# Seven products for pairs of MLP up tiles, and the down projection in groups of four hidden tiles

## The chip, the core and the metric

The kernel runs on one core of a Trainium2 chip. What counts is the device time of one execution in microseconds; three runs gave 1147.07, 1148.77 and 1148.97, the median being 1148.77. TensorE (PE in the rows) multiplies, VectorE (DVE) and ScalarE (ACT) work on tiles, GpSimd (POOL) on a few, and SyncE (SP) issues the loads and stores.

## The reference

An encoder trunk of two layers on 512 positions, 1024 channels wide, in float32. Each layer mixes (layer 0 by a gated convolution, layer 1 by differential attention over shared keys and values; both with a 4-head attention over a memory of 256 rows beside it), and then has an MLP of 4096 hidden channels:

```
def sqrelu_mlp(h, w_up, w_down):
    u = jnp.einsum('bsd,df->bsf', h, w_up)
    return jnp.einsum('bsf,fd->bsd', jnp.square(jax.nn.relu(u)), w_down)
...
        x = x + jnp.einsum('bse,ed->bsd', jnp.concatenate([main, mo], axis=-1), w_o[l])
        x = x + sqrelu_mlp(rmsnorm(x, norm_mlp[l]), w_up[l], w_down[l])
```

rmsnorm divides by the root of the mean square over the channels and multiplies by a gain.

## The kernel before

Everything lies transposed, channels on partitions and the 512 positions in the free dimension; the residual stream is 8 tiles x of 128 x 512. To keep float32 accuracy each operand is split into two halves of type fp32r, a rounded part and the rest (wh and wl for weights, xh and xl for activations, hh and hl for hidden tiles), and each product of 128 x 128 weights with a tile is three matmuls into the same PSUM bank: wh by xh, wh by xl, wl by xh (`product`, L276 to L281).

Weights come as a list of units (`_unit_list`), in the order of use, each of up to 8 blocks of 128 x 128. `dma_to` (L225) loads a unit into one of 3 buffers raw. `prep_to` (L251) splits a half unit of 4 blocks: ScalarE copies it to wh (L261), VectorE subtracts to wl (L263). It is called three halves ahead of the matmuls (AHEAD is 3), and there are 4 buffers of wh and of wl. `gemm_pieces` (L283) goes through the 8 blocks of a unit, 24 matmuls in all.

`mlp` (L737) works in 4 quarters of 8 hidden tiles. A quarter has 8 up projections and then 8 down projections:

```
                dve.scalar_tensor_tensor(out=v, in0=ps, scalar=0.0, in1=rstd, op0=ALU.max, op1=ALU.mult)
                act.activation(out=hh, in_=v, func=AF.Square)
                act.activation(out=a, in_=v, func=AF.Square)
                dve.tensor_tensor(out=hl, in0=a, in1=hh.bitcast(F32), op=ALU.subtract)
```

(L762 to L765) for each up tile, where rstd is the inverse root of the norm, applied behind the product; the norm's gain is in xh and xl already. A down unit accumulates the 8 hidden tiles of the quarter in one bank, and L772 adds it to x. At the end of the first MLP each x tile is split for the next layer and its square added up (`norm_tile` L430, `norm_square`; on GpSimd, the last one on VectorE: L455); the sum is split into ah and al (`norm_split`), and `norm_root` (L464) has TensorE add it over the partitions (L467, L468). In layer B the weights of attention are first multiplied by the norm's gain on GpSimd (L244).

The W_o stage of layer 0 adds to x (L882) and splits it for the MLP (L435, L436). In the second MLP the first two up tiles are done together (`side`). `mem_keys` and `mem_values` work on the 256 memory rows, thus with matmuls of 256 columns. PSUM's 8 banks are 3 for `gbank`, 1 in pn and 4 in pm_. The code gives each engine its instructions and the tile framework places them in the engines' queues: a queue's order is the framework's, which need not be that of the code.

Of the kernel before, what the change touches and what calls it, by code (L numbers as in the profile page):

```python
# [22 lines left out]
NF = 4  # L23
# [30 lines left out]

LAYER_B = ([(0, t) for t in range(6)] + [(1, t) for t in range(5)] + [(2, t) for t in range(4)]
# [8 lines left out]
def _unit_list():  # L64

    u = []
    u += [("qmA", t, KT) for t in range(2)]
    for m in range(NH):
        if m == MEMA:
            u += [("mkv", 0, t, KT) for t in range(4)]  # L70
        if m == MEMB:
            u += [("mkv", 1, t, KT) for t in range(4)]
        u += [("win", CONV + m * P, KT), ("win", 2 * CONV + m * P, KT), ("win", m * P, KT)]
    u += [("woA", d, KT) for d in range(KT)]

    def mlp(l):
        r = []
        for q in range(NF):
            r += [("up", l, q * KT + f, KT) for f in range(KT)]
            r += [("dn", l, q, d, KT) for d in range(KT)]  # L80
# [12 lines left out]
    return u  # L93
# [8 lines left out]
def _pack_weights(a_w_in, b_w_q, w_kv, w_mem_kv, w_o, w_up, w_down):  # L102
    wall = np.empty(OFFS[-1], np.float32)

    def cols(w, c0):
        return w[:, c0 : c0 + P].reshape(-1, P, P).transpose(1, 0, 2)

    for u, off in zip(UNITS, OFFS):
        kind = u[0]
        if kind == "qmA":  # L110
            b = cols(a_w_in[0], 3 * CONV + u[1] * P)
        elif kind == "win":
            b = cols(a_w_in[0], u[1])
        elif kind == "mkv":
            b = cols(w_mem_kv[u[1]], u[2] * P)
        elif kind == "woA":
            b = cols(w_o[0], u[1] * P)
        elif kind == "up":
            b = cols(w_up[u[1]], u[2] * P)
        elif kind == "dn":  # L120
            b = cols(w_down[u[1]][u[2] * D : (u[2] + 1) * D], u[3] * P)
# [12 lines left out]
        wall[off : off + n] = np.ascontiguousarray(b).reshape(-1)  # L134
    return wall
# [56 lines left out]
def trunk_kernel(ctx: ExitStack, tc: tile.TileContext, xT, memT, wall, cst, shp, csn, out):  # L192
# [11 lines left out]
    xspool = mk("xspool")  # L204
    hpool = mk("hpool", 8)
    qpool = mk("qpool", 16)
    ptpool = mk("ptpool")
# [10 lines left out]
    halves = [(i, h) for i, u in enumerate(UNITS) for h in range((u[-1] + SEG - 1) // SEG)]  # L218
# [6 lines left out]
    def dma_to(n, between=()):  # L225
        between = list(between)
        while st["dma"] <= min(n, len(UNITS) - 1):
            i = st["dma"]
            kind, nb = UNITS[i][0], UNITS[i][-1]
            r = wpool.tile([P, KT, P], F32, tag="raw", name="raw", bufs=3)  # L230
# [19 lines left out]

    def prep_to(n):  # L251
        while st["prep"] <= min(n, len(halves) - 1):
            i, h = halves[st["prep"]]
            dma_to(i + 1)
            r = st["raw"][i]
            b0, b1 = h * SEG, min(UNITS[i][-1], h * SEG + SEG)
            rs = r[:, b0:b1, :]
# [84 lines left out]
    def gbank():  # L342
        return pg.tile([P, S], F32, tag="g", name="g")
# [16 lines left out]

    def load_consts():
# [7 lines left out]
    def load_shape_consts():  # L369
        ind = tpool.tile([P, 512], F32, tag="att", name="ind", bufs=2)  # L370
# [59 lines left out]
    def norm_tile(k, src, g0, w, hi, lo, squares=True):  # L430
# [6 lines left out]
        if squares:  # L437
            norm_square(k, src, w)

    def norm_square(k, src, w, eng=None, by=None, tags=("sqf",)):  # L440
# [6 lines left out]
        if k == 0:  # L447
            nrm["acc"] = tpool.tile([P, S], F32, tag="vt", name="acc")
            square(nrm["acc"][:, :w])
        else:  # L450
# [3 lines left out]
            eng = eng or (dve if k == KT - 1 else pool)  # L454
# [87 lines left out]
    def mem_queries(hn, srcs, rstd, layer):  # L542
        def one(t):
            ps = gbank()
            yield from gemm_pieces(ps, srcs)
# [39 lines left out]
    def mem_attention(mq, mkk, mv, mixer, pace):  # L585
        def rest(T, hp, pr_):
            yield pace[1]
            th = ptpool.tile([P, 4, M], F32R, tag="p1h", name="mth")
            tl = ptpool.tile([P, 4, M], F32R, tag="p1l", name="mtl")
# [20 lines left out]
        for T in range(2):  # L610
            for hp in range(2):
# [9 lines left out]
                pr_ = tpool.tile([P, 4, M], F32, tag="att", name="mp", bufs=2)  # L621
# [35 lines left out]
    def diff_attention(p, qk, vv, mixer, done):  # L657
        obs, pts = {}, {}

        def rest(h, i, pm):  # L660
# [6 lines left out]
            if il == 0:  # L667
                th = ptpool.tile([P, nj, M], F32R, tag=f"p{T}h", name="th")
                tl = ptpool.tile([P, nj, M], F32R, tag=f"p{T}l", name="tl")
# [29 lines left out]
        def softmax(h, i, sc):  # L699
# [6 lines left out]
            pm = tpool.tile([P, 2, S], F32, tag="att", name="pm", bufs=2)  # L706
# [24 lines left out]

    def hid_pair():
        return (hpool.tile([P, S], F32R, tag="hh", name="hh"), hpool.tile([P, S], F32R, tag="hl", name="hl"))

    kept = []

    def mlp(l, xs, xs_next):  # L737
        rstd = new_rstd()
        parts = norm_split(S) if l == 0 else None
        for q in range(NF):  # L740
            hid = []
            ahead = {}
            for f in range(KT):
# [9 lines left out]
                if q == 0 and f == 0:  # L753
                    if parts is None:
                        for d in range(KT):
                            norm_square(d, x[d], S, tags=("sqf", "saf", "ob", "rp"))
                        parts = norm_split(S)
                    norm_root(parts, S, rstd)
                v = qpool.tile([P, S], F32, tag="q", name="v")
                a = qpool.tile([P, S], F32, tag="q", name="a")  # L760
                hh, hl = hid_pair()
                dve.scalar_tensor_tensor(out=v, in0=ps, scalar=0.0, in1=rstd, op0=ALU.max, op1=ALU.mult)  # L762
                act.activation(out=hh, in_=v, func=AF.Square)  # L763
                act.activation(out=a, in_=v, func=AF.Square)  # L764
                dve.tensor_tensor(out=hl, in0=a, in1=hh.bitcast(F32), op=ALU.subtract)  # L765
                hid.append((hh, hl))
            for d in range(KT):
                last = q == NF - 1 and xs_next is None
                for c in (slice(0, M), slice(M, S)) if last and d == KT - 1 else (slice(0, S),):
                    ps = gbank()  # L770
                    gemm(ps[:, c], hid, cols=c)
                    dve.tensor_tensor(out=x[d][:, c], in0=x[d][:, c], in1=ps[:, c], op=ALU.add)  # L772
                    if last:
                        nc.sync.dma_start(out=out[d * P : (d + 1) * P, c], in_=x[d][:, c])
                if q == NF - 1 and not last:
                    norm_tile(d, x[d], None, S, xs_next[d][0], xs_next[d][1])
                    kept.append(dpool.tile([P, S], F32, tag=f"x{d}", name=f"x{d}"))
                    nc.sync.dma_start(out=kept[d], in_=x[d])
# [100 lines left out]
    for d in range(KT):  # L879
# [3 lines left out]
        norm_tile(d, x[d], C_MLP0, S, xs[d][0], xs[d][1])  # L883
    lam_consts()
    xs_next = xs_tiles()
    mlp(0, xs, xs_next)


    xs = xs_next
    rstd = new_rstd()  # L890
# [5 lines left out]
    q0, q1 = mem_queries(hn, xs, rstd, 1)  # L896
# [125 lines left out]
    mlp(1, x_new, None)  # L1022
# [35 lines left out]
```

## Time and profile before

| | |
|---|---|
| median of three runs | 1148.77 us |
| the profiled execution | 1148.93 us, of which the span 1147.2 |
| TensorE matmuls | 5343, busy 1133.3 us (99%) |
| VectorE, ScalarE, GpSimd busy | 658.0 (57%), 535.2 (47%), 127.4 us (11%) |
| first MLP | 211.4 to 558.3 us |
| second MLP | 791.5 to 1145 us |

A row of a timeline has the start in the span, the duration, the engine and line, and what it writes and reads; in brackets, the idle time of the engine ahead of it and what ended that. A group row has the count, the busy time and the mean duration, and then the idle time before its members. Matmuls overlap: their durations don't add up, their starts do.

### The profile page before, as it was taken

To read this page: it belongs to the slowest core of one execution; us is meant where nothing else is said; L and a number is where in the kernel's file an instruction comes from. 1 tells how busy PE (TensorE), PEld (TensorE's weight loads), DVE (VectorE), ACT (ScalarE), POOL (GpSimd) and SP (SyncE) were. 2 spreads that over 40 slices of the span, in tenths; PEclk is the share of its full clock that TensorE was granted. 3 is DMA by queue.
4 is the path that set the end of the run, shared out by engine and by line. 5 is a ranking of instruction groups with operands and counts; after the bars stand their busy time and mean duration, and the time that the engine had idled before them with its cause. 6 is when DMAs were issued, how large, how long until landed. Compare 5 with 4: busy or idle time off the path is not lost.

```text
span 1147.2 us, 14439 instructions
## 1 busy us (share of the span) xinstructions
PE 1133.3 (99%) x5343; PEld 929.5 (81%) x5343; DVE 658.0 (57%) x1106; ACT 535.2 (47%) x1037; POOL 127.4 (11%) x130
## 2 busy tenths in 40 slices
PE   8999999999999999999999999999999999999998
PEld 6888888888888888888887777777788888888887
DVE  7876664653443443444678899977643443543442
ACT  6656544442342342344577777675532432432431
POOL 3100002000000000002523342224000000000000
PEclk9999999999999999999999999999999999999999
DMA  7232333223322322234322223212322232223231
GB/s 270 97 112 73 103 108 102 92 92 98 104 92 92 107 95 92 95 108 138 120 83 67 63 70 106 93 56 74 99 103 92 93 108 94 92 96 107 93 114 70
DMA packets 38983, 113.64 MB, mean 99 GB/s; under 512 B 4992, under 2 KB 6528, under 8 KB 38912
## 3 DMA queue, kind: packets, MB, share of 16 engines
q1 hardware_dynamic: 38912, 112.71, 29.8%
q8 instruction: 42, 0.69, 0.2%
q14 instruction: 29, 0.24, 0.1%
HBM read 106.93 MB, written 4.19 MB: 97 GB/s over the span
## 4 chain that ended last, share of the span: by engine, by line
PE 85%; DVE 4%; ACT 2%; issue 1%; ACTq 0%; DVEq 0%
PE g L279 26%; PE g L280 26%; PE g L281 26%; PE sc L583 1%; PE mov L603 1%; PE o L690 1%; DVE xl L436 1%; PE mtp L594 1%; DVE wl L263 1%; PE msc L583 0%; PE tp L677 0%; DVE ra L420 0%; DVE dnb L705 0%; DVE x L1018 0%; ACT pm L708 0%
## 5 line engine op out<-in xcount | busy, mean ns | idle before, releaser
L261 ACT ACTIVATE wh<-raw 128x512 fp32r<-128x512 f32 x384 | 241.8, 630 | 482.6 <-PE g L280 422.5
L263 DVE TENSOR_TENSOR wl<-raw,wh 128x512 fp32r<-128x512 f32 x370 | 263.4, 713 | 176.0 <-ACT wh L261 174.7
L279 PE MATMUL g<-xh,wh 128*128 128x512 f32 x816 | 323.4, 397 | 0.4 <-DVE x L1018 0.4
L280 PE MATMUL g<-xl,wh 128*128 128x512 f32 x816 | 320.4, 393 | 1.8 <-DVE xl L436 1.7
L281 PE MATMUL g<-xh,wl 128*128 128x512 f32 x816 | 319.0, 391 | 0.0
L279 PE MATMUL g<-hh,wh 128*128 128x512 f32 (+1 forms) x626 | 243.1, 388 | 0.0
L281 PE MATMUL g<-hh,wl 128*128 128x512 f32 (+1 forms) x626 | 242.2, 387 | 0.0
L280 PE MATMUL g<-hl,wh 128*128 128x512 f32 (+1 forms) x626 | 242.2, 387 | 0.0
L279 PEld LDWEIGHTS g<-xh,wh 128*128 128x128 f32 x816 | 153.9, 189 | 36.1 <-issue 2.5
L280 PEld LDWEIGHTS g<-xl,wh 128*128 128x128 f32 x816 | 153.9, 189 | 35.3 <-DVE xl L436 4.8
L281 PEld LDWEIGHTS g<-xh,wl 128*128 128x128 f32 x816 | 153.9, 189 | 32.2
L279 PEld LDWEIGHTS g<-hh,wh 128*128 128x128 f32 x626 | 117.7, 188 | 24.6 <-issue 0.9
L281 PEld LDWEIGHTS g<-hh,wl 128*128 128x128 f32 x626 | 117.7, 188 | 23.8
L280 PEld LDWEIGHTS g<-hl,wh 128*128 128x128 f32 x626 | 117.8, 188 | 23.4
L772 DVE TENSOR_TENSOR x<-x,g 128x512 f32<-128x512 f32 (+1 forms) x65 | 44.2, 680 | 105.3 <-PE g L281 105.3
L762 DVE SCALAR_TENSOR_TENSOR v<-g,rstd 128x512 f32<-128x512 f32 x64 | 44.2, 691 | 90.9 <-PE g L281 90.9
L455 POOL TENSOR_TENSOR acc<-acc,sqf 128x512 f32<-128x512 f32 x18 | 25.7, 1427 | 368.2 <-ACT sqf L443 367.8
L765 DVE TENSOR_TENSOR hl<-a,hh 128x512 fp32r<-128x512 f32 x64 | 44.3, 693 | 37.8 <-ACT a L764 37.8
L244 POOL TENSOR_TENSOR raw<-raw,cs 128x512 f32<-128x512 f32 x40 | 47.2, 1198 | 78.3 <-DMA raw<-in_wall_dram 47.4
L763 ACT ACTIVATE hh<-v 128x512 fp32r<-128x512 f32 x64 | 40.4, 632 | 19.3 <-DVE v L762 19.3
L764 ACT ACTIVATE a<-v 128x512 f32<-128x512 f32 x64 | 39.4, 615 | 0.0
L708 ACT ACTIVATE pm<-sc,dnb 128x128 f32<-128x128 f32 (+3 forms) x48 | 24.9, 521 | 9.3 <-DVE dnb L705 9.1
(284 smaller groups left out, 1024.0 us busy)
## 6 DMA issues: line engine op xcount, KB each, us to landing
raw<-in_wall_dram SPq DMA_DIRECT2D x170, 512.0 KB, 3.5
raw<-in_wall_dram SPq DMA_DIRECT2D x44, 256.0 KB, 3.0
x<-x SPq DMA_DIRECT2D x16, 256.0 KB, 2.5
x<-in_xT_dram SPq DMA_DIRECT2D x8, 256.0 KB, 5.0
out_dram<-x SPq DMA_DIRECT2D x7, 256.0 KB, 2.0
mraw<-in_memT_dram SPq DMA_DIRECT2D x4, 256.0 KB, 5.8
rc<-qp SPq DMA_DIRECT2D x24, 32.0 KB, 1.9
qp<-rc SPq DMA_DIRECT2D x24, 32.0 KB, 2.0
```

Source lines behind the costliest of these rows:

```text
L244: pool.tensor_tensor(out=rs, in0=rs, in1=cs[:, g0 + b0 : g0 + b0 + step].unsqueeze(2).to_broadcast([P, step, P]), op=ALU.mult)
L261: act.activation(out=wh[:, :n_, :], in_=rs, func=AF.Copy)
L263: eng.tensor_tensor(out=wl[:, :n_, :], in0=rs, in1=wh[:, :n_, :].bitcast(F32), op=ALU.subtract)
L279: pe.matmul(out=ps, lhsT=wh, rhs=xh, start=start, stop=False)
L280: pe.matmul(out=ps, lhsT=wh, rhs=xl, start=False, stop=False)
L281: pe.matmul(out=ps, lhsT=wl, rhs=xh, start=False, stop=stop)
L455: eng.tensor_tensor(out=acc, in0=acc, in1=sq, op=ALU.add)
L762: dve.scalar_tensor_tensor(out=v, in0=ps, scalar=0.0, in1=rstd, op0=ALU.max, op1=ALU.mult)
L763: act.activation(out=hh, in_=v, func=AF.Square)
L764: act.activation(out=a, in_=v, func=AF.Square)
L765: dve.tensor_tensor(out=hl, in0=a, in1=hh.bitcast(F32), op=ALU.subtract)
L772: dve.tensor_tensor(out=x[d][:, c], in0=x[d][:, c], in1=ps[:, c], op=ALU.add)
```

## The change

Of each layer's 32 hidden tiles the first 4 stay as they were. The other 28 are made in 14 pairs. For a pair the 1024 input channels are taken as 4 pairs of row blocks (even, odd) and the 512 positions as two halves of 256. Each 2 x 2 block product (two output tiles, two row blocks, two halves of the positions) is done by the seven products of Strassen's method, as Winograd orders its sums. Each of the seven adds up 4 products over the pairs of row blocks, with matmuls of 256 columns; sums and differences of weights are made in place in the raw buffers, those of activations (t1 to t4) once per layer by `seven_acts`, three of the four in the W_o stage in layer 0, all in the MLP in layer 1. The seven results are added on VectorE. Positions are swapped in one of the output pairs, so there is a swapped copy of rstd.

The hidden channels are now 8 groups of 512. Between two pairs stands half a down projection: four output tiles by the group's 4 hidden tiles, in four banks. Its two halves of output tiles alternate so that a bank is kept over two groups where it can be. Hidden tiles are kept by twos. The raw buffers are 4, not 3; tiles of attention share buffers with the new ones. In layer 1 the first memory queries take the row blocks in the order in which the first MLP now ends them (4 to 7, then 0 to 3).

```diff
+HALVES = ((0, 1), (1, 0))
+EVEN_ODD = (0, 2, 4, 6, 1, 3, 5, 7)
+SEVEN = ((0, "11", 0, 0), (1, "21", 1, 0), (2, "t4", 3, 1), (3, "t1", 2, 0), (4, "t2", 1, 1), (5, "t3", 2, 1), (6, "22", 3, 0))
...
+        r = [("up", l, f, KT) for f in range(4)]
+        for e in range(NE):
+            for n, h in enumerate(HALVES[e % 2]):
+                r += [("dn", l, e, h, kp, KT) for kp in range(2)]
+                if e < NE - 1:
+                    r += [("us", l, e * 4 + 4 + n * 2 + f, KT) for f in range(2)]
...
+    def seven_forms(i, h):
+        a11, a12 = (st["raw"][i][:, b : b + SEG, :] for b in (0, SEG))
+        a21, a22 = (st["raw"][i + 1][:, b : b + SEG, :] for b in (0, SEG))
+        if h == 3:
+            dve.tensor_tensor(out=a22, in0=a21, in1=a22, op=ALU.add)
+        elif h == 4:
+            dve.tensor_tensor(out=a21, in0=a11, in1=a21, op=ALU.subtract)
+            dve.tensor_tensor(out=a11, in0=a22, in1=a11, op=ALU.subtract)
+        elif h == 6:
+            dve.tensor_tensor(out=a12, in0=a12, in1=a11, op=ALU.subtract)
+        return (a11, a12, a22, a22, a11, a21, a12)[h]
...
+    def seven_acts(j, g0):
+        e, o = (qpool.tile([P, 2, M], F32, tag="q", name="xg") for _ in range(2))
+        for t, k in ((e, 2 * j), (o, 2 * j + 1)):
+            act.activation(out=t, in_=x[k].rearrange("p (c m) -> p c m", c=2), func=AF.Identity, scale=cs[:, g0 + k : g0 + k + 1])
+        t12, t34 = (qpool.tile([P, 2, M], F32, tag="q", name="tf") for _ in range(2))
+        for out_, a, b in ((t12[:, 0], e[:, 1], e[:, 0]), (t12[:, 1], o[:, 1], t12[:, 0]),
+                           (t34[:, 0], o[:, 1], e[:, 1]), (t34[:, 1], o[:, 0], t12[:, 1])):
+            dve.tensor_tensor(out=out_, in0=a, in1=b, op=ALU.subtract)
...
+            split(h[:, c : c + 2, :], l[:, c : c + 2, :], t)
...
+        def up_seven(f):
...
+            for n, (w_, x_, bank, half) in enumerate(SEVEN):
+                prep_to(first[(u, w_)] + AHEAD)
+                wh, wl = st["w"][(u, w_)]
+                for j in range(4):
+                    product(b[bank][:, half, :], (wh[:, j, :], wl[:, j, :]), forms[x_](j), j == 0, j == 3)
+                if n == 0:
+                    act.activation(out=p1, in_=b[0][:, 0, :], func=AF.Copy)
+                if n == 4:
+                    plus(qa, twice(p1), b[1])
+                if n == 5:
+                    plus(qb, twice(qa[:, 1, :]), b[2])
+                    plus(qa[:, 1, :], qb[:, 1, :], b[2][:, 0, :])
+            plus(qc, qb, b[3])
+            for t, r, at in ((qa, rstd, slice(0, 4, 3)), (qc, swap, slice(1, 3))):
+                t = t.rearrange("p c m -> p (c m)")
+                dve.scalar_tensor_tensor(out=t, in0=t, scalar=0.0, in1=r, op0=ALU.max, op1=ALU.mult)
+                hidden(f, t, at)
+        def down(e, h, n):
+            fin = e == NE - 1
+            begin, end = n == 1 or e == 0, n == 0 or fin
...
+            for kp in range(2):
...
+                for i in range(4):
...
+                            product(ps[:, c], w, [t[:, k, c] for t in hid[e * 2 + p_]],
+                                    begin and p_ == 0 and k == 0, end and p_ == 1 and k == 1)
+                        if not (end and kp == 1):
+                            continue
+                        dve.tensor_tensor(out=x[d][:, c], in0=x[d][:, c], in1=ps[:, c], op=ALU.add)
...
+        up_plain()
+        for e in range(NE):
+            for n, h in enumerate(HALVES[e % 2]):
+                down(e, h, n)
+                if e < NE - 1:
+                    up_seven(e * 4 + 4 + n * 2)
```

`hidden` is the two squares and the difference hl of L763 to L765; `up_plain` is the old loop over four tiles, and `plus` an addition on VectorE of a PSUM bank to a tile.

## Rows read from the trace of the kernel before

**Rows 1.** The page: busy time, share and instructions by engine, and of the 40 slices of the span the busy tenths of TensorE, VectorE and the DMA engines and the granted clock.

```profile
PE 1133.3 (99%) x5343; PEld 929.5 (81%) x5343; DVE 658.0 (57%) x1106; ACT 535.2 (47%) x1037; POOL 127.4 (11%) x130
PE   8999999999999999999999999999999999999998
DVE  7876664653443443444678899977643443543442
PEclk9999999999999999999999999999999999999999
DMA  7232333223322322234322223212322232223231
```

**Rows 2.** Busy time by stage: start and end, its length, then busy us (instructions) of TensorE, its weight loads, VectorE, ScalarE and GpSimd, the granted clock, the DMA share and GB/s. The stages are W_o of layer 0, the first MLP, layer B, and W_o's end with the second MLP.

```profile
168.80:211.40 42.60, 42.60 (x189) 35.28 (x189) 23.09 (x34) 20.45 (x33) 8.01 (x6) 1.00 0.31 99
211.40:558.30 346.90, 346.90 (x1531) 287.27 (x1531) 159.42 (x235) 127.77 (x210) 17.31 (x14) 1.00 0.31 102
558.30:798.00 239.70, 233.61 (x1230) 184.16 (x1229) 198.63 (x411) 171.97 (x400) 78.59 (x81) 0.99 0.25 78
```

**Rows 3.** Groups by line, shapes apart: count, busy us, mean ns, idle time before.

```profile
L279 PE MATMUL g<-xh,wh 128*128 128x512 f32 x816 | 323.4, 397 | 0.4 <-DVE x L1018 0.4
L279 PE MATMUL g<-mxh,wh 128*128 128x256 f32 x64 | 18.1, 283 | 0.0
L263 DVE TENSOR_TENSOR wl<-raw,wh 128x512 fp32r<-128x512 f32 x370 | 263.4, 713 | 176.0 <-ACT wh L261 174.7 <-PE mtp L594 0.6
L765 DVE TENSOR_TENSOR hl<-a,hh 128x512 fp32r<-128x512 f32 x64 | 44.3, 693 | 37.8 <-ACT a L764 37.8
L762 DVE SCALAR_TENSOR_TENSOR v<-g,rstd 128x512 f32<-128x512 f32 x64 | 44.2, 691 | 90.9 <-PE g L281 90.9
```

**Rows 4.** Timeline of TensorE in the first MLP, the first and the last of 55 starts of 512 columns.

```profile
318.06 0.39 PE L279 MATMUL g<-xh,wh 128*128 128x512 f32 x1
...
330.30 0.39 PE L279 MATMUL g<-xh,wh 128*128 128x512 f32 x1
```

**Rows 5.** Timeline of TensorE and its weight loads (PEld) in mem_keys, the first and the last of 31 starts of 256 columns.

```profile
57.10 0.28 PE L279 MATMUL g<-mxh,wh 128*128 128x256 f32 x1
57.10 0.19 PEld L280 LDWEIGHTS g<-mxl,wh 128*128 128x128 f32 x1
...
60.70 0.28 PE L279 MATMUL g<-mxh,wh 128*128 128x256 f32 x1
60.70 0.19 PEld L280 LDWEIGHTS g<-mxl,wh 128*128 128x128 f32 x1
```

**Rows 6.** Timeline of all engines at the end of an up unit of the first MLP.

```profile
321.24 0.39 PE L281 MATMUL g<-xh,wl 128*128 128x512 f32 x1
...
321.66 0.69 DVE L762 SCALAR_TENSOR_TENSOR v<-g,rstd 128x512 f32<-128x512 f32 x1 [1.54 <-PE g L281]
322.27 0.69 DVE L263 TENSOR_TENSOR wl<-raw,wh 128x512 fp32r<-128x512 f32 x1
...
322.39 0.63 ACT L763 ACTIVATE hh<-v 128x512 fp32r<-128x512 f32 x1 [0.26 <-DVE v L762]
322.93 0.61 ACT L764 ACTIVATE a<-v 128x512 f32<-128x512 f32 x1
323.57 0.69 DVE L765 TENSOR_TENSOR hl<-a,hh 128x512 fp32r<-128x512 f32 x1 [0.62 <-ACT a L764]
```

**Rows 7.** VectorE's order at the start of the second MLP (x2: two in a row); and instructions by tile or line with their first and last start.

```profile
810.67 1.28 DVE L762 SCALAR_TENSOR_TENSOR v<-g,rstd 128x512 f32<-128x512 f32 x2
812.57 0.69 DVE L765 TENSOR_TENSOR hl<-a,hh 128x512 fp32r<-128x512 f32 x1 [0.62 <-ACT a L764]
...
L392 ACT ACTIVATE rope<-rope,cs x2: 710/710/711, 32.4 to 33.0; 128x512 f32<-128x512 f32 x2
...
L882 DVE TENSOR_TENSOR x<-x,g x8: 686/688/689, 168.8 to 206.9; 128x512 f32<-128x512 f32 x8
```

**Rows 8.** The page's DMA issues: count, KB each, median us from issue to landing.

```profile
raw<-in_wall_dram SPq DMA_DIRECT2D x170, 512.0 KB, 3.5
```

**Rows 9.** Busy time by stage at the start of the second MLP, and TensorE's wait there.

```profile
791.50:815.40 23.90, 22.16 (x92) 16.45 (x91) 21.40 (x27) 15.42 (x28) 8.85 (x6) 1.00 0.29 93
815.40:826.30 10.90, 10.90 (x49) 9.02 (x49) 6.15 (x10) 5.60 (x10) 0.00 (x0) 1.00 0.34 115
...
805.29 0.50 PE L467 MATMUL ss<-ah,onesr 128*128 128x512 f32 x1 [1.02 <-ACT ah L346]
```

**Rows 10.** Timeline at the end of the first MLP.

```profile
549.32 2.04 POOL L244 TENSOR_TENSOR raw<-raw,cs 128x512 f32<-128x512 f32 x2 [0.58 <-DVE wl L263]
...
552.10 1.56 POOL L455 TENSOR_TENSOR acc<-acc,sqf 128x512 f32<-128x512 f32 x1 [0.74 <-ACT sqf L443]
...
555.38 0.39 PE L279 MATMUL g<-xh,wh 128*128 128x512 f32 x1
...
556.19 1.51 DVE L263 TENSOR_TENSOR wl<-raw,wh 128x512 fp32r<-128x512 f32 x1
...
558.93 0.63 ACT L346 ACTIVATE ah<-acc 128x512 fp32r<-128x512 f32 x1 [0.23 <-DVE acc L455]
...
559.60 0.69 DVE L347 TENSOR_TENSOR al<-acc,ah 128x512 fp32r<-128x512 f32 x1
...
560.83 0.40 PE L467 MATMUL ss<-ah,onesr 128*128 128x512 f32 x1
```

More of the change, by code (lines that the diff above doesn't have):

```diff
@@ L119, in _pack_weights @@
             b = cols(w_up[u[1]], u[2] * P)
+        elif kind == "us":
+            b = cols(w_up[u[1]], u[2] * P)[:, EVEN_ODD, :]
         elif kind == "dn":
-            b = cols(w_down[u[1]][u[2] * D : (u[2] + 1) * D], u[3] * P)
+            _, l, e, h, kp, _ = u
+            rows = [w_down[l][(e * 4 + kp * 2 + k) * P :][:P] for k in range(2)]
+            b = np.stack([rows[k][:, d * P : (d + 1) * P] for d in range(h * 4, h * 4 + 4) for k in range(2)], axis=1)
         elif kind == "qB":
@@ L215, in trunk_kernel @@
     ptr = po = psc = pm_
-    halves = [(i, h) for i, u in enumerate(UNITS) for h in range((u[-1] + SEG - 1) // SEG)]
+    halves = []
+    for i, u in enumerate(UNITS):
+        if u[0] != "us":
+            halves += [(i, h) for h in range((u[-1] + SEG - 1) // SEG)]
+        elif u[2] % 2 == 0:
+            halves += [(i, h) for h in range(len(SEVEN))]
     side = next(i for i, u in enumerate(UNITS) if u[:2] == ("up", 1))
@@ L437, in norm_tile, with norm_square @@
         if squares:
-            norm_square(k, src, w)
-    def norm_square(k, src, w, eng=None, by=None, tags=("sqf",)):
+            norm_square(k, src, w, **kw)
+    def norm_square(k, src, w, eng=None, by=None, tags=("sqf",), first=0, last=KT - 1):
         def square(out):
@@ L539, in mkv_pair, with mem_queries @@
         return (mpool.tile([P, S], F32R, tag="m", name="mh"), mpool.tile([P, S], F32R, tag="m", name="ml"))
-    def mem_queries(hn, srcs, rstd, layer):
+    def mem_queries(hn, srcs, rstd, layer, order=range(KT)):
         def one(t):
             ps = gbank()
-            yield from gemm_pieces(ps, srcs)
+            yield from gemm_pieces(ps, srcs, order=order)
             qn = qn_tile(layer)
@@ L752, in mlp @@
                     gemm(ps, xs)
-                if q == 0 and f == 0:
-                    if parts is None:
+                if f == 0:
+                    pt = parts
+                    if pt is None:
                         for d in range(KT):
                             norm_square(d, x[d], S, tags=("sqf", "saf", "ob", "rp"))
-                        parts = norm_split(S)
-                    norm_root(parts, S, rstd)
+                        pt = norm_split(S)
+                    norm_root(pt, S, rstd)
+                    for c in range(2):
+                        act.activation(out=swap[:, c * M : c * M + M], in_=rstd[:, M - c * M : S - c * M], func=AF.Copy)
@@ L766, in mlp @@
[L766 to L778, printed above, removed]
+                hidden(f, v, slice(f % 2 * 2, f % 2 * 2 + 2))
@@ new lines, in up_plain, with plus, twice @@
+                if f not in sev:
+                    seven_acts(f, g0)
+        def up_seven(f):
+            u = cur["u"]
+            cur["u"] += 2
+            b = [psc.tile([P, 2, M], F32, tag="misc", name="us") for _ in range(4)]
+            forms = {"11": lambda j: [t[:, 0:M] for t in xs[2 * j]], "21": lambda j: [t[:, 0:M] for t in xs[2 * j + 1]],
+                     "22": lambda j: [t[:, M:S] for t in xs[2 * j + 1]]}
+            for n in range(4):
+                forms[f"t{n + 1}"] = lambda j, n=n: [t[:, n, :] for t in sev[j]]
+            hid[f // 2] = hid_tile("hh"), hid_tile("hl")
+            qa, qb, qc = (qpool.tile([P, S], F32, tag="q", name="c").rearrange("p (c m) -> p c m", c=2) for _ in range(3))
+            p1 = tpool.tile([P, M], F32, tag="sqf", name="p1")
+            def plus(out, a, ps):
+                dve.tensor_tensor(out=out, in0=a, in1=ps, op=ALU.add)
+            def twice(a):
+                return a.unsqueeze(1).to_broadcast([P, 2, M])
+            for n, (w_, x_, bank, half) in enumerate(SEVEN):
[15 more added lines that the diff above has]
+                hidden(f, t, at)
```

111 lines of the change are left out of this document (76 added, 35 removed).

## The prediction

> **What bounds the kernel now.** I read the page's busy line and slices first. TensorE is busy 1133.3 of 1147.2 us, at a granted clock of 9 tenths or more in every slice, and its digit never falls under 8; VectorE is at 57%, with 3 to 5 tenths inside the two MLPs [rows 1]. The stage table says the same: from 211.4 to 558.3, the first MLP, TensorE has no idle time at all, while VectorE works 159 and ScalarE 128 of 347 us [rows 2]. So the time is the number of matmuls times the step from one start to the next; a matmul's own 390 ns overlap with the next one's [rows 3]. That step is read from starts. In an up projection the first and the last of 55 starts (54 steps) are 318.06 and 330.30: 12.24 / 54 = 0.2267 us for 512 columns [rows 4]. In the stream of 256-column matmuls, each with weights of its own, 30 steps take 60.70 - 57.10 = 3.60: 0.1200 us [rows 5]. Half the columns cost 53%, not 50%.
>
> **The products.** A pair of up tiles over 8 row blocks took 2 x 8 x 3 = 48 matmuls of 512: 10.88 us. Seven products over 4 pairs of row blocks are 7 x 4 x 3 = 84 of 256: 10.08 us. That is 0.80 us, 7.4%, per pair and not an eighth. Of 32 hidden tiles per layer, 4 stay plain, so 14 pairs per layer, 28 in all: -22.4 us. The down projection keeps its 768 matmuls per layer; only their order changes. Its last tile, cut in halves, saves 0.2 us, which I leave out. From the profiled run's 1148.93 us (span 1147.2 and 1.73 around it; the median of the three runs is 1148.77) the products alone give 1126.5.
>
> **What VectorE and ScalarE get.** I count one cycle of 512 hidden columns: two downs of 48 full matmuls (10.88 us each) and two sevens (10.08): 41.9 us of TensorE. A seven gives VectorE 4 sums of raw weights, 7 wl, qa, qb, a half qa and qc, two v and two hl: 18 operations of 512 elements and one of 256. A down has 4 wl, and every other down 4 additions to x. Independent operations start 0.61 us apart (v at 321.66, wl at 322.27 [rows 6]), so a cycle is 2 x 11.4 + 2 x 2.4 + 2.4 = 30.0 us, 72% of 41.9; at the full durations of 0.69 to 0.71 [rows 3] it is 34.8, 83%. Before, the same work was 28 operations, 17 us in 43.5. ScalarE gets 7 wh, the copy p1 and 4 squares per seven, some 17 us per cycle at its 0.54 step [rows 6]: it doesn't bind. Throughput thus hides the new work, if VectorE doesn't sit waiting for ScalarE: sum, wh, wl is a round trip of about 0.79 us (0.04 + 0.63 + 0.04, and 0.08 of lost overlap), three times per seven, and hl waits 1.3 us behind its v, twice [rows 6]. In the order of the code, with nothing in between, that is 5.0 per seven: 40.0 us per cycle at the best step, 44.8 at full durations. The bounds of this term are then nothing, and 44.8 - 41.9 = 2.9 us per cycle, 41 us over 14 cycles.
>
> I take nothing, because the engines' order isn't that of the code. The code has the hl of a tile before the v of the next, but VectorE ran two v's and then the first hl (810.67, 812.57), and the rope scaling, which the code puts behind the W_o stage, ran at 32.4 while that stage's additions run from 168.8 [rows 7]. The waits are thus filled with work that is ready.
>
> **The tightest wait.** In each cycle the second seven makes hidden tiles that the next down needs after its first 24 matmuls, 5.44 us on (5.67 for the matmul that reads hl). Behind the last product: 0.2 until VectorE starts, qc 0.69, its v 0.69, two squares 1.2, hl 0.69: 3.5 us with the hand-overs, the other half (qa) being complete one product earlier. With two other operations in front it is 4.7, in time. In the code's order (qa's v, squares and hl ahead of qc's) it is 5.9, with 0.2 of backlog 6.1: 0.45 us late, 14 times, 6 us. Inside a seven, weights are prepared three products ahead. In the code's order behind a down with additions, counted from the seven's start: the last addition to x ends at 0.9, sum, wh and wl of the fourth product at 2.9, two sums, wh and wl of the fifth at 5.5, wl of the sixth at 6.1, sum, wh and wl of the seventh at 8.1; that one is read at 8.9 (six products of 1.44 and two matmuls). PSUM doesn't add a wait: a down holds four banks, which are read out one seven (10 us) before the next down begins in them. SP's queue only issues loads, in the same bytes: the next pair's first block takes the buffer that the last wl of a seven frees, about 7 to 8 us into it; with 3.5 us to landing [rows 8] it is there by 12 and used at 12.8. If that slack were gone, wh, wl and their matmuls would wait, but the page's DMA rows are at 3 tenths [rows 1].
>
> **The edges.** In the W_o stage of layer 0 three preparations of activations (4 differences of 0.42, two splits of 0.69: 3.06 us of VectorE each) meet 19.5 us of idle VectorE in 42.6 [rows 2]: nothing. At the start of the second MLP all four (12.2 us) come where VectorE is busy 21.4 of 23.9 us and TensorE already stands 1.0 for ah [rows 9]. They are first read some 3 us into the first seven; until then VectorE is free 2.5 us, then about 8.5 in the first down, then 1: 12.0 against 12.2, with nothing to spare. Between 0 and the 6 us that half of them would cost, I take 1.5. At the end of the first MLP the last four x tiles come 1.36 us apart instead of 5.44. The sum of squares (the square of the first of the four is ready 2.0 us before the last matmul; then three additions on GpSimd at 1.56, a weight scaling of 2.0 among them, one addition on VectorE, ah and al) ends 6.8 us after the last matmul. Before, it ended 4.9 us after it (555.38 to 560.29), and the matmul of ah, at 560.83, didn't wait [rows 10]. The matmul of al, due at 5.7, is 1.1 late; between 0 and 2.5 (VectorE at the 1.51 of a wl beside GpSimd [rows 10]) I take 1.0. Sum: 1126.5 + 2.5 = **1129.0 us**.
>
> **A rule that speaks against it.** The rows above have 226.7 and 120.0 ns. The Trainium skill, TensorE: Matmul & The Clock Gate, section Back-to-back issue gap, gives a sustained stream of weight load and matmul about 131 ns at 512 columns and 81 ns at 128; between them, as an estimate, 98 ns at 256. By that a pair would cost 48 x 131 = 6.3 before and 84 x 98 = 8.2 us after, and the change would lose 1.9 us x 28 = 54 us. The trace disagrees at both sizes and decides.
>
> **The rivals.**
> (A) VectorE becomes the bound, because its order leaves the waits unfilled. For: its load per cycle goes from 17 to 30 us, and each round trip to ScalarE is there now as 0.62 us of idle time before hl [rows 6]. Against: rows 7, and the 30% of it that stay free. At full durations, 2.9 us per cycle: 1129.0 + 41 = 1170. It decides from 20 / 14 = 1.4 us per cycle, where the gain is gone; around there the time is 1147 to 1151.
> (B) The code's order holds only at the tight wait, 6 us, and the edges cost their upper ends, 6 more: 1129 + 12 = 1141; still faster.
> (C) A matmul of 256 columns behind its own weight load costs more than half by much. The load's row is 0.19 us; were loads in a row not overlapped, 84 x 0.19 = 16.0 against 10.88, 5.1 x 28 = +143: 1272. Against it: two loads there start 57.10 and 60.70, 30 matmuls apart, so 0.12 each [rows 5]. The skill's rule above, with its +54, is of this kind.
> (D) The fourth weight buffer also serves layer B, where TensorE stands 6.1 us of 239.7 [rows 2]: 1123 at the best, inside the forecast's range.
>
> **How the numbers follow.** Forecast (with D), 1121 to 1136: 0.62. B, 1136 to 1146: 0.15. A, slower, 1151 to 1175: 0.17; A at its turning point: 0.04. C: 0.02. Range 1121 to 1150, which leaves out most of A and C. Something under 0.2% (2.3 us) can't be told from no change here. Faster 0.77, same 0.04, slower 0.19.
>
> **What would show it.** TensorE's count rises by 28 x 36 less 12 in the last tile, to 6339. A seven's matmuls start 0.120 us apart without holes, 10.1 us for 84; the first MLP's 347 us become 336. VectorE is at 7 tenths and over in the MLPs, yet no wait of TensorE for hl, wl or sh stands high in the list of waits. I am wrong if TensorE waits for hl or wl in each cycle (A, B), or if the step at 256 columns is over 0.125 us.

## The result and the profile after

The kernel after takes 1138.37 us (median of four runs, 1137.58 to 1140.11) where the kernel before took 1147.92 beside it: the ratio is 0.9919, with an interval of 0.9902 to 0.9937. That is 9.5 us faster. The sign and the wide range hold, the size doesn't: the forecast was 1129.0, a gain of 20, and 1138 lies outside the likeliest case (1121 to 1136). The forecast starts from the profiled run of before, 1148.93, which is 1.0 above the median here; between the two profiled runs the spans differ by 11.4 us, and the sums below go by those.

The page of the kernel after; these lines answer to [rows 1]:

```profile
span 1135.8 us, 17096 instructions
PE 1116.3 (98%) x6339; PEld 960.1 (85%) x6339; DVE 878.3 (77%) x1470; ACT 610.0 (54%) x1185; POOL 129.5 (11%) x130
...
PE   8999999999999999999899999999999999999998
...
DVE  7876667777787777778868898977988678678775
...
PEclk9999999999999999999899999999999999999999
```

TensorE has the 6339 matmuls that were counted, VectorE went from 57% to 77% and stands at 7 and 8 tenths in the first MLP, mostly at 6 to 8 in the second. There is one new dent: in slice 20 both TensorE and its clock show an 8. A slice is 28.4 us, so that is 540 to 568, the end of the first MLP.

Inside the first MLP all came as forecast. First its row of the busy time by stage (columns as in [rows 2]), then the timeline of TensorE at the first product of a seven, at its last, and at the down that follows:

```profile
210.00:546.00 336.00, 336.00 (x2035) 301.97 (x2034) 256.23 (x394) 155.66 (x267) 17.01 (x15) 1.00 0.33 105
```

```profile
302.68 0.28 PE L311 MATMUL us<-xh,wh 128*128 128x256 f32 x1
...
312.63 0.28 PE L313 MATMUL us<-xh,wl 128*128 128x256 f32 x1
312.75 0.40 PE L311 MATMUL g<-hh,wh 128*128 128x512 f32 x1
```

TensorE is busy 336.0 of 336.0 us, and the 84 matmuls of a seven take 312.75 - 302.68 = 10.07 us. From ss, which opens the MLP (212.14 before, 212.01 after), to layer B's first matmul (555.38 [rows 10], 544.55 after) it is 343.24 and 332.54 us: 10.7 shorter, of 11.2 forecast.

Then most of that is lost. Layer B opens with the memory queries, which begin 10.8 us earlier than before; its first qk result is read out only 2.7 us earlier (573.5 and 570.8). Busy time by stage at this edge, before and then after, same columns:

```profile
544.00:552.00 8.00, 8.00 (x37) 6.60 (x37) 6.12 (x7) 4.19 (x7) 6.23 (x5) 1.00 0.38 127
```

```profile
544.00:552.00 8.00, 6.26 (x26) 4.30 (x24) 7.94 (x8) 3.83 (x7) 7.26 (x5) 1.00 0.52 184
552.00:560.00 8.00, 5.11 (x12) 3.40 (x12) 6.16 (x7) 3.62 (x6) 2.92 (x4) 0.60 0.33 112
```

VectorE is busy 7.94 of 8 us and GpSimd 7.26, and TensorE begins to stand; over the next 8 us its granted clock is 0.60 in the mean. Line numbers differ from kernel to kernel by what was put in. The waits of TensorE there (us in total, times, longest) and the timeline of its long ones:

```profile
PE g L312 <- DVE xl L379: 2.2, 2, 1.5
PE ss L506 <- DVE al L379: 1.4, 1, 1.4
PE ss L505 <- ACT ah L378: 0.8, 1, 0.8
PE g L311 <- ACT xh L378: 0.2, 1, 0.2
```

```profile
548.40 0.39 PE L313 MATMUL g<-xh,wl 128*128 128x512 f32 x1
...
551.00 0.50 PE L312 MATMUL g<-xl,wh 128*128 128x512 f32 x1 [1.52 <-DVE xl L379]
...
556.42 0.79 PE L506 MATMUL ss<-al,onesr 128*128 128x512 f32 x1 [1.43 <-DVE al L379]
...
560.42 0.41 PE L313 MATMUL g<-xh,wl 128*128 128x512 f32 x1
560.68 0.39 PE L311 MATMUL g<-xh,wh 128*128 128x512 f32 x1
```

Between 548.40 and 560.68 there are 18 steps from start to start; at 0.2267 they are 4.08 us, and they took 12.28: 8.2 us lost. Nine of them, 556.42 to 560.42, took 4.00 instead of 2.04: 2.0 of the 8.2 are the lower clock, the rest are waits and the restarts behind them. And this is what VectorE and GpSimd did meanwhile (timeline of both):

```profile
546.14 1.52 DVE L379 TENSOR_TENSOR xl<-x,xh 128x512 fp32r<-128x512 f32 x1
547.59 0.68 DVE L903 TENSOR_TENSOR x<-x,g 128x512 f32<-128x512 f32 x1
...
548.78 1.56 DVE L295 TENSOR_TENSOR wl<-raw,wh 128x512 fp32r<-128x512 f32 x1
550.27 0.68 DVE L379 TENSOR_TENSOR xl<-x,xh 128x512 fp32r<-128x512 f32 x1
551.01 1.63 DVE L379 TENSOR_TENSOR xl<-x,xh 128x512 fp32r<-128x512 f32 x1
...
554.85 1.52 DVE L379 TENSOR_TENSOR al<-acc,ah 128x512 fp32r<-128x512 f32 x1
```

```profile
545.63 2.94 POOL L262 TENSOR_TENSOR raw<-raw,cs 128x512 f32<-128x512 f32 x2
548.53 1.27 POOL L493 TENSOR_TENSOR acc<-acc,sqf 128x512 f32<-128x512 f32 x1
550.53 1.55 POOL L493 TENSOR_TENSOR acc<-acc,sqf 128x512 f32<-128x512 f32 x1 [0.74 <-ACT sqf L481]
```

GpSimd scales the weights of layer B (L262) and adds squares (L493). The differences xl, wl and al, with both inputs in SBUF, mostly take 1.5 to 1.7 us beside it and not 0.69, while the addition of a PSUM bank to x, beside the same scaling, stays at 0.68. Not each one is longer: the xl of 550.27 starts before GpSimd's addition of 550.53 and takes 0.68. The others start while GpSimd works, and wl and the next xl end 0.54 and 0.56 us after its instruction does (549.80 to 550.34, 552.08 to 552.64): what they pay is about the rest of that instruction.

The theory is then: four x tiles now come 1.36 us apart, VectorE has no time to spare, and GpSimd nearly doubles the time of what it must do for them. Its rivals: ScalarE held up by its single buffer for squares; the sum of squares alone; the spacing of the tiles alone. The first of the runs below on this edge (plain pairs, four buffers, root later) were made for another theory, in which the close tiles and ScalarE's buffer were to blame; GpSimd's price to VectorE was put on record after them.

### The profile page after: what moved, and what is told of

Read it like the earlier page. It is cut to its first block, busy times and chain, and to the rows that moved or that the text cites. A ratio compares the mean times of both kernels' runs of the same rounds, so it can differ in the third digit from the quotient of the medians.

```text
span 1135.8 us, 17096 instructions
## 1 busy us (share of the span) xinstructions
PE 1116.3 (98%) x6339; PEld 960.1 (85%) x6339; DVE 878.3 (77%) x1470; ACT 610.0 (54%) x1185; POOL 129.5 (11%) x130
## 4 chain that ended last, share of the span: by engine, by line
PE 85%; DVE 8%; ACT 3%; issue 1%; POOL 1%; DMA 0%; SPq 0%; DVEq 0%; ACTq 0%; POOLq 0%
PE g L311 15%; PE g L312 15%; PE g L313 15%; PE us L313 8%; PE us L311 8%; PE us L312 8%; PE dn L311 2%; PE dn L312 2%; PE dn L313 2%; DVE wl L295 1%; PE sc L621 1%; PE mov L641 1%; PE o L728 1%; DVE xl L474 1%; PE msc L621 1%
## 5 line engine op out<-in xcount | busy, mean ns | idle before, releaser
L312 PE MATMUL g<-xl,wh 128*128 128x512 f32 x368 | 147.1, 400 | 3.8 <-DVE xl L379 2.2
L311 PE MATMUL g<-xh,wh 128*128 128x512 f32 x368 | 150.0, 408 | 0.8 <-DVE x L1159 0.4
L312 PE MATMUL g<-hl,wh 128*128 128x512 f32 x384 | 149.9, 390 | 0.0
L313 PE MATMUL g<-hh,wl 128*128 128x512 f32 x384 | 149.5, 389 | 0.0
L311 PE MATMUL g<-hh,wh 128*128 128x512 f32 x384 | 149.4, 390 | 0.0
L313 PE MATMUL g<-xh,wl 128*128 128x512 f32 x368 | 145.3, 395 | 0.0
L311 PE MATMUL us<-sh,wh 128*128 128x256 f32 x448 | 127.1, 284 | 0.8 <-ACT wh L293 0.8
L313 PE MATMUL us<-sh,wl 128*128 128x256 f32 x448 | 126.8, 283 | 0.2 <-DVE wl L295 0.2
L312 PE MATMUL us<-sl,wh 128*128 128x256 f32 x448 | 126.8, 283 | 0.0
L313 PE MATMUL us<-xh,wl 128*128 128x256 f32 x336 | 95.1, 283 | 0.0
```

Source lines behind the costliest of these rows:

```text
L311: pe.matmul(out=ps, lhsT=wh, rhs=xh, start=start, stop=False)
L312: pe.matmul(out=ps, lhsT=wh, rhs=xl, start=False, stop=False)
L313: pe.matmul(out=ps, lhsT=wl, rhs=xh, start=False, stop=stop)
```

## The experiments

**Whose edge is it?** Pairs plainly, in the new order of units with its new downs:

```diff
-                    r += [("us", l, e * 4 + 4 + n * 2 + f, KT) for f in range(2)]
+                    r += [("up", l, e * 4 + 4 + n * 2 + f, KT) for f in range(2)]
...
-                    up_seven(e * 4 + 4 + n * 2)
+                    up_two(e * 4 + 4 + n * 2)
```

> The pairs are computed plainly (48 matmuls of 512 columns each), the down projection stays in its new order, no sums of weights, activations or results. Theory (late tiles, an effect of the down order alone): the matmuls cost 22.4 us more, the 1.5 us at the second MLP's start are not lost, and the 8.4 us at the first MLP's end and 0.8 at the last tile stay lost: 1138.4 + 22.4 - 1.5 = 1159, and slower than before by 9 to 10. Rival (VectorE's new load from the sevens makes the tiles late): the edge is as before and the time is that of before, 1148 to 1151.

Measured: 1157.46 us, ratio 1.0083 [1.0068, 1.0098]. TensorE waits at the edge for xl 2.2, al 1.4, xh 0.5 and ah 0.5 us, as after. So the loss belongs to the order of the downs and not to the seven products, which by themselves bring 1157.5 - 1138.4 = 19 us: 22.4 less the 1.9 that they cost at the second MLP's start (below) is 20.5, the same to within the spread of the runs.

**ScalarE's buffer.** Four buffers for the squares instead of one:

```diff
-                        norm_tile(d, x[d], None, S, xs_next[d][0], xs_next[d][1], first=LATE[0], last=LATE[-1])
+                        norm_tile(d, x[d], None, S, xs_next[d][0], xs_next[d][1], first=LATE[0], last=LATE[-1], tags=("sqf", "saf", "ob", "rp"))
```

> Theory (late tiles): the changed kernel's last four x tiles of the first MLP come 1.36 us apart, the GpSimd additions of squares (1.3 to 1.7 us each, weight scalings of 2.0 to 2.9 us between them) can't keep that pace, and with one buffer for the squares ScalarE's next square waits for them and holds the xh behind it. With four buffers for the squares the xh and xl of the last tiles come in time: TensorE's waits for xh and xl there, 2.4 us in the trace, vanish, the first wait for the sum stays, the half-clock stretch gets shorter; 2 to 5 us off 1138.4, 1134 to 1136. Rival (sum only): what holds TensorE is the sum of squares alone, whatever ScalarE's queue does; then the time stays within 1 us of 1138.4.

Measured: 1137.45 us, 0.9907 [0.989, 0.9925], no change from after. ScalarE no longer waits for GpSimd's additions, and TensorE waits for xl as long as after, now in one piece (waits of TensorE, 520 to 600):

```profile
PE g L312 <- DVE xl L379: 2.6, 1, 2.6
PE ss L506 <- DVE al L379: 0.6, 1, 0.6
```

It was the theory of this run, and it fell.

**The sum alone.** The root, with the matmuls of ah and al, four blocks later:

```diff
+    for _ in range(4):
+        next(q1)
     norm_root(parts, S, rstd)
```

> The matmuls that add up the squares are placed four blocks (2.7 us) later, into the second memory query. Theory (late tiles): the waits for xh and xl stay, of the 2.2 us of waits for ah and al most goes, the clock falls for a shorter time: 1 to 4 us off 1138.4. Rival (sum only): the whole 8 us of the edge is this wait and the clock that falls after it: 5 us and more off, 1133 or below.

Measured: 1138.0 us, 0.9913 [0.9898, 0.9927]. The waits for ah and al are gone, those for xl stay (2.4 us), and later steps of the chain wait instead (hss and bc of the norms of the heads, 0.6 each). So it isn't the sum alone either, and the 1 to 4 us that were expected didn't come: what is late is all of VectorE's work.

**The spacing.** The last group of the first MLP finishes each x tile at once, 2.72 us apart instead of 1.36:

```diff
+            halves[j : j + 4] = [(i, 0), (i + 1, 0), (i, 1), (i + 1, 1)]
...
+                    whole = tail or (fin and not last)
...
+                        blocks = [(p_, k) for p_ in ((0, 1) if whole else (kp,)) for k in range(2)]
```

> In the last group of the first MLP each output tile is finished before the next begins, so the last four x tiles come 2.72 us apart and not 1.36; nothing else changes. Theory (spacing): VectorE gets 8.2 us instead of 4.1 for the last four tiles' work; most of the 8.4 us of this edge comes back, 1131 to 1134. Rival (the edge is slow because the weight scalings for layer B and their loads fall into it, whatever the spacing): less than 2 us off 1138.4.

Measured: 1140.25 us, 0.9941 [0.9921, 0.996]; its interval meets that of after, so no gain, perhaps a loss. TensorE waits for ah 2.8, xh 1.7 and xl 1.1 us, and GpSimd is busy 7.84 of the 8 us from 544 to 552. More space alone doesn't help.

**Less for GpSimd.** The additions of squares on VectorE instead:

```diff
-                        norm_tile(d, x[d], None, S, xs_next[d][0], xs_next[d][1], first=LATE[0], last=LATE[-1])
+                        norm_tile(d, x[d], None, S, xs_next[d][0], xs_next[d][1], first=LATE[0], last=LATE[-1], eng=dve)
```

> At the first MLP's end the seven additions of squares go to VectorE, none to GpSimd (10 us less there, some 4.3 us more on VectorE at 0.61). Theory (VectorE beside GpSimd: its operations on two SBUF tiles take 1.5 us instead of 0.69 while GpSimd works, so VectorE has no time left at this edge): the wl and xl beside the former additions fall back to 0.69, VectorE gains more than it takes on; TensorE's waits there shrink and the time falls by 2 to 5 us, to 1133 to 1136. Rival (VectorE has no time left because it has too many operations): with 7 more the waits for xl grow, 1140 and over.

Measured: 1135.67 us, 0.9894 [0.9872, 0.9915]. VectorE has more to do and yet TensorE waits less (xl 0.9, al 0.6), at full clock. Group of the xl (count, shortest/median/longest ns), of this kernel from 536 to 558 and then of after:

```profile
L379 DVE TENSOR_TENSOR xl<-x,xh x6: 677/680/1525, 538.5 to 552.3; 128x512 fp32r<-128x512 f32 x6
```

```profile
L379 DVE TENSOR_TENSOR xl<-x,xh x6: 677/1338/1724, 537.1 to 551.0; 128x512 fp32r<-128x512 f32 x6
```

The intervals of the two kernels overlap, so the 2.7 us are not settled by the times; the halved median of xl is, and so is the edge in the traces (table below).

**The scalings left out.** The first eight weight units of layer B are not scaled:

```diff
-                if kind in ("qB", "kv", "qk", "kk"):
+                if kind in ("qB", "kv", "qk", "kk") and i >= qb + 8:
```

> The scaling by the norm's gain is left out for the first 8 weight units of layer B, so GpSimd has only the additions of squares at the first MLP's end. Theory (VectorE beside GpSimd): VectorE's wl and xl in the stretch lose the 1.5 us durations for the greater part, and 2 to 5 us come back, to 1133 to 1136. Rival (spacing alone, whatever GpSimd does): the last tiles stay late, less than 2 us off.

Measured: 1131.69 us, 0.9866 [0.9847, 0.9886], 6.7 less than after, clear of its interval, and more than the 2 to 5 us that were expected. Busy time by stage, the waits of TensorE, and VectorE's timeline:

```profile
544.00:552.00 8.00, 6.93 (x29) 4.90 (x28) 7.76 (x11) 5.17 (x9) 3.50 (x3) 1.00 0.45 155
552.00:560.00 8.00, 8.00 (x35) 6.39 (x36) 5.60 (x9) 4.39 (x8) 0.00 (x0) 1.00 0.20 66
```

```profile
PE ss L507 <- ACT ah L380: 0.8, 1, 0.8
PE ss L508 <- DVE al L381: 0.2, 1, 0.2
```

```profile
544.76 0.68 DVE L381 TENSOR_TENSOR xl<-x,xh 128x512 fp32r<-128x512 f32 x1
...
551.08 0.69 DVE L381 TENSOR_TENSOR al<-acc,ah 128x512 fp32r<-128x512 f32 x1
```

In the same 8 us VectorE gets through 11 instructions instead of 8. The waits for xl are gone, the clock stays at 1.00, and what is left are waits of 1.0 us for ah and al. This shows the cause of most of the edge: GpSimd's scalings beside VectorE. That the weights only became usable earlier doesn't explain it: in after, no wait of TensorE at this edge is for wh or wl, and VectorE itself hardly waits (busy 7.94 of 8 us).

**The scalings moved.** ScalarE has idle time there (4.2 and 4.4 us of 8 after). It scales the first eight units of layer B, or, in a second kernel, only the fourth to the seventh, each with four activations per half unit; both kernels also give the second half of the last tile a bank of its own (below):

```diff
+                    if qb + 0 <= i < qb + 8:
+                        for b in range(b0, b0 + step):
+                            act.activation(out=r[:, b, :], in_=r[:, b, :], func=AF.Copy, scale=cs[:, g0 + b : g0 + b + 1])
+                    else:
+                        pool.tensor_tensor(
```

> The gain is put on layer B's first 8 weight units by ScalarE, 4 scaled copies in place per half unit, instead of by GpSimd; and the last tile's second half has a bank of its own. Theory (GpSimd's scalings slow VectorE at the first MLP's end): VectorE is freed as in the run without scalings, which took 1131.7; ScalarE takes on some 16 x 1.2 us over 40 us and stays under 90%; with the 0.8 of the bank 1130 to 1134. Rival (leaving out the scalings only helped because loads became usable earlier, not because of VectorE): ScalarE's scaling delays them as GpSimd's did, 1136 to 1139.

> As the run before, but only the units 4 to 7 of layer B, whose scaling falls between the first MLP's last tiles and the norm's root, are scaled by ScalarE. Theory: the scalings that stand beside the last four tiles decide, those before them do not; within 1.5 us of the run with eight units. Rival (all of GpSimd's work in the last 30 us counts): 2 us and more over it.

Measured: 1133.28 us, 0.9871 [0.9854, 0.9887], and 1133.96 us, 0.9874 [0.9859, 0.9889], both clear of the interval of after. Eight or four make no difference, which speaks for the units scaled beside the last four x tiles. These two are the shortest versions that leave nothing out: 4 to 5 us less than after, 0.8 of which is the bank. A part of the edge is still there; the second kernel by stage:

```profile
544.00:552.00 8.00, 6.78 (x28) 4.67 (x26) 7.23 (x10) 6.83 (x15) 4.36 (x3) 1.00 0.74 248
552.00:560.00 8.00, 7.01 (x30) 5.35 (x29) 5.88 (x10) 8.00 (x24) 0.00 (x0) 1.00 0.23 80
```

ScalarE is now full, 8.00 of 8 us.

**The edge in the traces.** Each profiled run gives the edge by itself, without the rest of the kernel: from the start of layer B's first matmul to that of the 100th behind it, and to the end of al, with which the sum of squares is complete (us).

| kernel | to the 100th matmul | to the end of al |
|---|---|---|
| before | 23.26 | 4.9 |
| after | 31.39 | 11.8 |
| plain pairs | 31.80 | 12.2 |
| four buffers for squares | 31.21 | 11.2 |
| root later | 29.69 | 12.6 |
| tile by tile | 33.53 | 13.4 |
| additions of squares on VectorE | 27.39 | 10.7 |
| scalings left out | 25.13 | 7.4 |
| eight scalings on ScalarE | 27.15 | 8.1 |
| four scalings on ScalarE | 27.01 | 9.1 |

The scalings are worth 6.3 us of the 8.1 by which after is longer than before. What the later root wins here is lost again in layer B: up to the second MLP's ss it is 258.1 us, and 257.6 in after. Taking the additions of squares from GpSimd wins 4.0, so GpSimd's work counts here whichever it is. The nine differences of VectorE in question (four xl, the four wl among them, and al) took 12.0 us in after and 7.7 with four scalings on ScalarE.

**How much VectorE can still take.** Seven, then eleven additions more per seven, of which nothing else in the kernel depends:

```diff
+                for _ in range(1 if n % 2 else 2):
+                    dve.tensor_tensor(out=extra, in0=rstd, in1=swap, op=ALU.add)
```

(That is eleven; for seven, `else 1`.)

> Each seven gets 7 more additions of 128x512 on VectorE that nobody reads: 14 per cycle of 41.9 us, 8.5 us at a step of 0.61, so by my count VectorE works 38.5 us per cycle. Theory (VectorE's queue fills its waits, throughput decides): no more than 0.3 us per cycle, 0 to 4 us over 14 cycles, 1138 to 1143. Rival (the waits for ScalarE are not filled, VectorE is near its end already at 77% of the span): TensorE waits for wl and hl in each cycle, 2 us and more per cycle, 1166 and over.

> Each seven gets 11 more additions on VectorE that nobody reads, 22 per cycle: 30.0 + 13.4 = 43.4 us of VectorE for 41.9 us of TensorE. Theory (VectorE's queue fills its waits, its throughput decides): TensorE waits 1.5 us per cycle and more, 14 cycles: 1158 to 1170, with VectorE over 9 tenths in the MLPs; that puts VectorE's margin per seven between 7 and 11 operations. Rival (VectorE has more to spare than the count of 0.61 per operation says): under 1150.

Measured: 1143.26 us, 0.997 [0.9955, 0.9984], and 1161.9 us, 1.0123 [1.0108, 1.0138]. Busy time by stage with seven and with eleven more:

```profile
352.00:394.00 42.00, 42.00 (x266) 38.00 (x265) 41.64 (x70) 18.85 (x33) 0.00 (x0) 1.00 0.31 101
```

```profile
352.00:394.00 42.00, 42.00 (x266) 38.02 (x265) 41.74 (x71) 18.94 (x32) 0.00 (x0) 1.00 0.32 101
```

VectorE is full there in both, at 42 / 70 = 0.60 us per instruction; over 210 to 546 it is busy 306.8 us with seven and 326.5 with eleven, of 336. In the first MLP of after it is free 336.0 - 256.2 = 79.8 us: 7 x 14 x 0.60 = 59 us fit, 11 x 14 x 0.60 = 92 don't. With seven, TensorE has no wait in the first MLP (210 to 540), and of the 4.9 us some 2.8 are lost at the second MLP's start, where the granted clock falls to 0.50 (836 to 838); the time is 0.3 over what was expected. With eleven it waits for hh and wh all through the second MLP (7 and 8 times), and the gain is gone. One limit: these additions depend on nothing in a seven, so the queues could run them early. They test the amount of work and not a delay within the chain.

**The two small edges.** A bank for the second half of the last tile:

```diff
+                        if tail and c.start:
+                            ps = gbank()
```

> The second half of the very last tile gets a PSUM bank of its own. Theory (the first half's addition to x reads the bank that the second half's first matmul writes, so TensorE stood 0.8 us): 0.8 off, the hole of 0.8 between the halves is gone. Rival (the hole is the last weights' preparation): no change, the hole stays.

Measured: 1137.67 us, 0.9915 [0.9896, 0.9935]: not told apart from after by time, but the hole is gone from TensorE's starts. After had it here (timeline of VectorE, then TensorE):

```profile
1130.60 0.42 DVE L903 TENSOR_TENSOR x<-x,dn 128x256 f32<-128x256 f32 x1 [0.74 <-PE dn L313]
```

```profile
1130.28 0.28 PE L313 MATMUL dn<-hh,wl 128*128 128x256 f32 x1
1131.08 0.39 PE L311 MATMUL dn<-hh,wh 128*128 128x256 f32 x1 [0.51 <-DVE x L903]
```

And at the second MLP's start one preparation of activations instead of four:

```diff
+                if l == 1 and f > 0:
+                    sev[f] = sev[0]
+                elif f not in sev:
                     seven_acts(f, g0)
```

> In the second MLP only the first of the four preparations of activations is made and serves for all four, so the other three (9.2 us of VectorE) are left out and the products there are of other values. Theory (the holes in the first seven of the second MLP, 1.5 us more than before, are VectorE's backlog from these preparations): they vanish, 1.0 to 2 us off 1138.4. Rival (they are the first sums of weights waiting for their loads): the holes stay, no change.

Measured: 1136.88 us, 0.9901 [0.9886, 0.9916], a difference from after that the intervals don't settle. By stage, after and then this kernel:

```profile
823.00:834.00 11.00, 9.95 (x68) 8.87 (x67) 10.93 (x20) 5.44 (x10) 0.00 (x0) 1.00 0.00 1
```

```profile
823.00:834.00 11.00, 11.00 (x88) 10.73 (x87) 9.56 (x16) 4.70 (x8) 0.00 (x0) 1.00 0.25 94
```

VectorE's full 10.93 of 11 us become 9.56, and TensorE, which lost 1.9 us from start to start between 825 and 850, loses nothing.

## Why the prediction was right in the middle and wrong at the edge

**The products: right.** -22.4 us was forecast; the first MLP gave 10.7 of its 11.2, at 10.07 us per seven. The trace of before had the step at 256 columns, and it held. Rival C is out. In the second MLP 13 of the 14 sevens take 10.07 too; from its ss to the last matmul it is 338.56 us before and 330.36 after, and with the 1.9 and 0.8 that its start and its last tile lose, the products gave 10.9 there.

**VectorE's load: right.** 30.0 us per cycle were forecast, it is busy 31.8 of 42 (310 to 352 in the trace after). It has room for seven more operations per seven, not for eleven: VectorE can become the bound, but what rival A needs for it, waits that stay unfilled, was not there.

**The tightest wait: right, by the queue's order.** VectorE's timeline behind the seven that ends at 312.75:

```profile
313.65 0.69 DVE L873 SCALAR_TENSOR_TENSOR c<-c,rstd 128x512 f32<-128x512 f32 x1
314.25 0.69 DVE L873 SCALAR_TENSOR_TENSOR c<-c,rsw 128x512 f32<-128x512 f32 x1
...
316.15 1.29 DVE L809 TENSOR_TENSOR hl<-c,hh 128x512 fp32r<-128x512 f32 x2 [0.62 <-ACT c L808]
```

Both v run first, then both hl, as [rows 7] suggested and not as the code says. The last hl ends at 317.44, 4.7 us behind the last product, as forecast, and 1.0 before it is read (318.45). Rival B's first half is out. That 1138 lies within B's bounds is chance: its 6 us at this wait are not there, and the first MLP's end costs over three times B's upper end for it.

**The second MLP's start: right.** 1.5 us taken, 1.9 measured.

**The first MLP's end: the step that failed.** The prediction has the sum of squares complete 6.8 us after the last matmul, the matmul of al 1.1 late, and takes 1.0 us, "between 0 and 2.5 (VectorE at the 1.51 of a wl beside GpSimd [rows 10])". The sum was complete after 11.8 us, and 8.2 us were lost. What the prediction left out is that the price which it knew for one wl falls on nearly all differences that VectorE makes there: three of the last four xl (1.15, 1.52 and 1.63), the wl between them, and al. So the waits are not for the sum at the end alone but for xl before it, which has no term in the prediction, and 2.0 us of lower clock, which has none either. Without the scalings the sum is complete after 7.4 us and the edge costs 2.0 from start to start (1.0 of waits), within the 0 to 2.5 of the forecast. The trace of before had the price on an xl too, where 5.44 us between tiles hid it:

```profile
546.09 1.50 DVE L347 TENSOR_TENSOR xl<-x,xh 128x512 fp32r<-128x512 f32 x1
```

The rows show work of VectorE with two SBUF inputs at double length beside GpSimd, and PSUM additions untouched. The Trainium skill, SBUF — State Buffer, section Who interferes with whom, says why: VectorE's second SBUF input goes through a read port that it shares with GpSimd, so an operation with two SBUF inputs contends with a GpSimd instruction that reads SBUF, and one with at most one, outside the modes that use both ports, doesn't. The trace agrees (xl, wl and al at 1.52, 1.56 and 1.52 against 0.68 for the additions to x); by that rule every difference at this edge, and not one, would have been open to the price.

**Not priced.** The last tile's halves share a bank: 0.8 us. Rival D brought little: between the first query read out and the second MLP's ss the lead over before goes from 2.7 to 3.2 us (ss at 805.29 and 802.13), 0.5 of the 6.1 that were to be had.

The sum, with what was forecast for each term:

| | forecast | measured |
|---|---|---|
| products (0.2 of the last tile not counted) | -22.4 | -21.6 (10.7 and 10.9) |
| end of the first MLP | +1.0 | +8.2 |
| start of the second MLP | +1.5 | +1.9 |
| last tile | 0 | +0.8 |
| layer B | 0 | -0.5 |
| sum | -19.9 | -11.2 (the span: -11.4; the medians: -9.5) |

## What to carry to other kernels

When an order is changed, take the stage where the new pace meets other engines' work, write down each helper operation there with the duration that it has in that neighbourhood, and add them up against the new spacing; an average duration of the stage hides a price that was paid under cover until now. The body of such a change can be forecast from starts and loads to half a microsecond, and the edges deserve as much of the working as the body. Where GpSimd works beside a full VectorE, look first for another engine for GpSimd's work.

## What the hardware showed that was not expected

- GpSimd's price to VectorE is on operations with both inputs in SBUF alone: 0.69 became 1.15 to 1.74 us, with PSUM additions at 0.68 in the same microseconds. It is no fixed price: an operation that starts while GpSimd works ends some 0.55 us after GpSimd's instruction (0.54 and 0.56 above), and one that started first (xl at 550.27, GpSimd at 550.53) keeps its 0.68. Moving the additions of squares from GpSimd to VectorE, more work for the engine that was full, made the waits shorter (xl 2.2 to 0.9 us).
- Short waits cost twice. TensorE's clock (granted level, the last but two of the columns) in after:

```profile
552.00:553.50 1.50, 0.73 (x2) 0.30 (x2) 1.36 (x3) 1.15 (x2) 0.32 (x2) 1.00 0.68 247
553.50:554.00 0.50, 0.00 (x0) 0.00 (x0) 0.50 (x1) 0.49 (x1) 0.50 (x1) 0.64 0.02 8
554.00:560.00 6.00, 4.38 (x10) 3.10 (x10) 4.30 (x5) 1.98 (x4) 2.11 (x3) 0.50 0.27 87
```

It fell between 553.5 and 554 to the lower level (1.2 of 2.4 GHz), after waits of 1.5 and 0.7 us and within the one of 0.8; the wait of 1.4 came when it was down. From 557.0 to 560.4 a step took 0.43 us instead of 0.227, 2.0 us more. With the additions on VectorE, without the scalings, and with four scalings on ScalarE the clock stayed at 1.00 there. Fewer waits are no guarantee: with eight scalings on ScalarE none was longer than 0.8 us (0.7, 0.8 and 0.3 between 549 and 553), and the level fell too, to 0.79 in the mean:

```profile
552.00:560.00 8.00, 7.74 (x27) 5.96 (x27) 4.63 (x7) 6.51 (x20) 0.00 (x0) 0.79 0.20 66
```

What decides when it falls is not shown here.
